# Up-projection: the products A22 T4 of a pair of sets made by seven inner products

## The chip, the cores and the metric

The kernel runs on one core of a Trainium2 chip. The metric is the device time of one launch in microseconds; less is better. On the core, TensorE (PE) multiplies; VectorE (DVE), ScalarE (ACT) and GpSimd (POOL) do elementwise work; SyncE (SP) issues nearly all the transfers.

## The reference

One inference step of a one-layer encoder in float32 on 1024 prompt frames and 32 new ones, 1056 columns in all. The part that the change touches is the up-projection of the squared-ReLU MLP:

```python
f = jnp.square(jax.nn.relu(rmsnorm(x, g_ffn) @ w_up)) @ w_down   # D_MODEL 1024, D_FF 4096
x = x + f
```

## The kernel before

Activations lie with channels on the 128 partitions and the 1056 columns along them. A float32 product is made of three matmuls on rounded values: every operand is split into a high part (a cast on ACT, `copy`) and a low part (source less high part, a subtraction on VectorE), and the kernel adds high x high, high x low and low x high.

**Sets and sevens.** The 4096 outputs of the up-projection are 16 sets of 256. A set's product is a 2 x 2 block product: outputs in two halves of 128, the 1024 inputs in two halves of 512 (four tiles of 128 each), the columns in two halves of 528. It is made from seven block products instead of eight: A11 B11, S1 T1, S2 T2, S3 T3, S4 B22, A12 B21 and A22 T4, where the S are sums of weight blocks (made by GpSimd in `prepare`, split on ACT and VectorE) and the T are sums of activation blocks, made and split once. Each block product runs in two quarters of the columns (264), 12 matmuls a quarter: 4 input tiles x 3. Results gather in PSUM banks: a bank that held A11 B11 is copied out (p1), S2 T2 is added into it, it is copied out again (u2), S3 T3 is added, the difference to S1 T1 (s5) is taken (m2), and A22 T4 is added. VectorE and ACT make the blocks m1 and m2 from the banks; then come Relu, square, a store (`mdB`), and sums of blocks for the down-projection (`mid_sums`: tiles ta and tb, stores to `mdT`).

**Pairs.** Sets 0 and 1 run alone (`seven_late`, `seven`). Sets 2 to 15 run as seven pairs (`seven_pair`). Of a pair one of the seven, A12 B21, is taken for both sets together, and as it is again a 2 x 2 block product (two sets, two halves of the inputs, two quarters), it too is made by seven inner products (`inner_product`, 6 matmuls each: 2 tiles x 3) in place of 48 matmuls. The activations for that, `inner_t` and `low_t`, stay in SBUF. The other six products of both sets take 12 x 2 quarters each, so a pair has 6 x 48 + 42 = 330 matmuls of 264 columns.

**What sets the order.** It is written out by hand. Every product yields when its matmuls are emitted, and `run` then takes one step of each generator in `side`: `prepare` for the next sets (each with a table of steps at which a cast stands; its low part follows a step later), `prepare_inner`, the hooks behind a finished block (`up_hooks`: Relu, square, store, sums), the loads. An engine takes its instructions in the order emitted, so what stands ahead on VectorE, ACT or SP and waits holds up all behind it. Activation tiles come from one pool `blk` of 37 buffers; a new tile waits until all reads of its buffer's last tile are done, transfers from it among them.

Names that the text uses: shS2/slS2 are the high and low part of S2; `raw_u9r` a weight tile of set 9; `td[k]` the DRAM copy of T(k+1), from which the fetches `rt` bring T3 and T4 back at set 0.

Of the kernel before, what the change touches and what calls it, by code (L numbers as in the profile page):

```python
# [15 lines left out]
P = 128  # L16
# [59 lines left out]
def tile_step(  # L76
# [109 lines left out]
        nc.scalar.copy(d[:, 0, :], src)  # L186
        dve(d[:, 1, :], src, d[:, 0, :].bitcast(F32), op=sub)

    def half_w(src, name):
        h, l = (wpool[0].tile([P, 4, P], F32R, tag=f"s{x}", name=f"s{x}{name}", bufs=SHB) for x in "hl")  # L190
        nc.scalar.copy(h, src)  # L191
        return (h, l), partial(dve, l, src, h.bitcast(F32), op=sub)

# [62 lines left out]
    def prepare_inner(key, odd):  # L256
# [38 lines left out]
        low()  # L295
        yield

    def inner_operands(name, g, load):
# [48 lines left out]

    def inner_product(name, w, b, p_=None, pool_=None):

        o = {"B11": low_t[0][0], "B21": low_t[1][0], "B22": low_t[1][1]}.get(b) or inner_t[b]  # L350
        new = p_ is None
        if new:
            p_ = group(f"ps_in{name}", TQ, pool_)
        on = dict(skip_group_check=not new)
        wh, wl = w
        for k in range(2):
# [120 lines left out]
                done("near")  # L477
        done("21")

    def seven_pair(s0, s1, key, m, last, after=({}, {})):  # L480

        def tile_of(k, i):
            return wpool[0].tile([P, TQ], F32, tag=k, name=f"{k}_{s0}{i}")
# [13 lines left out]
        def done(i, k):  # L497
            after[i].get(k, int)()
# [27 lines left out]
        def sixth(i, t):  # L526
            product(i, "A22", "T4", t, x[i][t])
            last(m(i, 1), q[t][1], x[i][t])

        for f in (first, second, third, fourth):  # L530
            for t in range(2):
                f(0, t)
                yield
# [39 lines left out]
        for f, ts_, k in ((third, (1, 0), ""), (fourth, (1, 0), "22"), (fifth, (0, 1), "12")):  # L573
            for t in ts_:
                f(1, t)
                yield
            done(1, k)
        for t in (1, 0):
            sixth(1, t)
            yield  # L580
            done(1, "near" if t else "21")
        for k in (s0, s1, key):
            ws.pop(k)

# [15 lines left out]
            partial(fetch_second, f"{nm}{b}r", w, nb),  # L600
        )

    def ahead_of(nm, a, n):

        e, o = f"{nm}{a}e", f"{nm}{a}o"
        return after(n, prepare(f"{nm}{a}", (6, 8, 10, 11, 14, 16), (e, o, 0))), after(n + 3, prepare_inner(f"{nm}{a}y", o))

    def pair_side(nm, a, b, then=None):

        order = ("S1", "A11", "S2", "S3", "S4", "A22")  # L610
        side.append(after(3, prepare(f"{nm}{b}", (4, 6, 8, 10, 13, 15), (f"{nm}{a}e", f"{nm}{a}o", 1), order)))
        if then:
            for n, f in zip((6, 8, 10, 19), pair_loads(nm, *then)):
                side.append(after(n, call(f)))
            side.extend(ahead_of(nm, then[1], 14))

    def run(body):

# [172 lines left out]
    def md(k, s_):  # L791
# [8 lines left out]
    cvd = dpool.tile([4, 2, P, T], F32, name="cvd")  # L800
    ed = dpool.tile([KD, P, T], F32, name="ed")
    edt = dpool.tile([P, 2, 2 * P], F32, name="edt")
    inner_s = {
        (k, p): {a: dpool.tile([P, NP_, P], F32, name=f"di{k}{p}{a}") for a in ("S1", "S2", "S3", "S4")}
        for k in NESTED for p in range(2)
# [938 lines left out]
        dve(tb[:, 0, :], m2[:, a], ta[:, 1, :], op=sub)  # L1744
        nc.sync.dma_start(md("T4", s_), tb[:, 0, :])

    def up_hooks(i, s_, m):

        def later_(*fs):
            for f in fs:  # L1750
# [31 lines left out]
    def up_pair(a, b):  # L1782
        ms = {}

        def m(i, j):
            if (i, j) not in ms:
                ms[i, j] = blk(f"m{j + 1}_{(a, b)[i]}")
            return ms[i, j]

        return seven_pair(  # L1790
            f"u{a}", f"u{b}", f"u{a}y", m, relu2, [up_hooks(i, (a, b)[i], partial(m, i)) for i in range(2)]
        )

    def up_source(a, b):
# [781 lines left out]
```

## Time and profile before

| | |
|---|---|
| runs | 1510.48, 1510.98 and 1512.48 us, median 1510.98 |
| the profiled execution | 1510.11 us |
| its span, first to last instruction | 1508.4 us |
| mean granted TensorE clock | 0.999 |
| matmuls in the trace | 11556 |
| up-projection, sets 2 to 15 | 789.05 to 1072.76 us, seven pairs of about 40.3 us |

All times of instructions and windows are microseconds from the span's start. In a row of a window stand, behind its bounds, its length; then for PE, PE's weight loads (PEld), DVE, ACT and POOL the busy time with the count of instructions; then the granted clock (1.00 is full), the share of the transfer engines and GB/s. In an order in time a row has start, duration, engine, line, operation, output and inputs, and in brackets idle time ahead of it with what ended it. In a row of a group stand busy time, mean ns and idle time ahead of it; in a row of transfers the count, KB of each and the median time from issue to landing.

### The profile page before, as it was taken

What the parts mean: (1) busy time and instruction counts of PE and PEld (TensorE: products, weight loads), DVE (VectorE), ACT (ScalarE), POOL (GpSimd) and SP (SyncE); (2) the same over time, 40 slices, a digit from 0 to 9 for tenths busy, and PEclk for the clock granted to TensorE, in tenths of its full rate; (3) what the DMA queues carried; (4) which work ended last, traced back from release to release, by engine and by line L of the source; (5) the groups of instructions that cost most, each with busy time, mean ns of one, the idle gap of its engine ahead of it and who ended that gap; (6) DMA issues with size and microseconds to landing.
All of it is one profiled execution on the core that took longest, in us unless ns stands there. A gap on an engine that the chain in (4) does not pass through costs nothing.

```text
span 1508.4 us, 29451 instructions
## 1 busy us (share of the span) xinstructions
PE 1495.6 (99%) x11556; PEld 1481.3 (98%) x11556; DVE 1149.1 (76%) x1628; ACT 794.6 (53%) x1575; POOL 377.7 (25%) x330
## 2 busy tenths in 40 slices
PE   9999999999999999999999999999999999999997
PEld 9999999999999999999999999999999999999997
DVE  6867788879578989876786676666688878879766
ACT  7654444445467767433475555555655433334655
POOL 0434334444121222003324333332000000000251
PEclk9999999999999999999999999999999999999999
DMA  6624425423688766655644434444979767855443
GB/s 242 213 74 171 169 57 198 156 84 98 226 265 251 199 157 154 221 181 184 230 151 146 148 129 144 157 157 150 322 280 284 245 192 238 289 185 166 142 129 123
DMA packets 117259, 275.52 MB, mean 183 GB/s; under 512 B 14048, under 2 KB 31072, under 8 KB 117120
## 3 DMA queue, kind: packets, MB, share of 16 engines
q1 hardware_dynamic: 112144, 259.39, 50.9%
q0 software_dynamic: 1728, 6.29, 2.5%
q10 hardware_dynamic: 3248, 7.96, 1.6%
q8 instruction: 91, 1.49, 0.4%
q14 instruction: 48, 0.39, 0.1%
HBM read 196.10 MB, written 85.88 MB: 187 GB/s over the span
## 4 chain that ended last, share of the span: by engine, by line
PE 93%; DVE 4%; issue 1%; ACT 1%; DMA 1%; ACTq 0%; DVEq 0%; SPq 0%
PE ps_dn L2016 6%; PE ps_dn L2015 6%; PE ps_dn L2014 6%; PE ps_A11i L374 5%; PE ps_A11i L373 5%; PE ps_A11i L375 5%; PE ps_A11u L374 4%; PE ps_A11u L373 4%; PE ps_A11u L375 4%; PE av L1294 2%; PE ps_S1i L375 2%; PE ps_S1i L374 2%; PE ps_S1i L373 2%; PE ps_wo L135 2%; PE ps_wo L133 2%; PE ps_wo L134 2%
## 5 line engine op out<-in xcount | busy, mean ns | idle before, releaser
L2016 PE MATMUL ps_dn<-fhP,wlo_dn 128*128 128x264 f32 x768 | 218.9, 285 | 0.0
L2015 PE MATMUL ps_dn<-flP,whi_dn 128*128 128x264 f32 x768 | 218.7, 285 | 0.1
L2014 PE MATMUL ps_dn<-fhP,whi_dn 128*128 128x264 f32 x768 | 218.2, 284 | 0.0
L2015 PEld LDWEIGHTS ps_dn<-flP,whi_dn 128*128 128x128 f32 x768 | 144.4, 188 | 0.4 <-DVE flP L1880 0.4
L2016 PEld LDWEIGHTS ps_dn<-fhP,wlo_dn 128*128 128x128 f32 x768 | 144.6, 188 | 0.2 <-DVE wlo_dn L1864 0.2
L2014 PEld LDWEIGHTS ps_dn<-fhP,whi_dn 128*128 128x128 f32 x768 | 144.6, 188 | 0.0
L1239 DVE TENSOR_TENSOR_SCAN r<-r 128x128 f32<-128x128 f32 (+3 forms) x64 | 86.8, 1356 | 5.3 <-POOL r L1232 5.3
L2229 POOL TENSOR_TENSOR xx<-xx,pgs 128x400 f32<-128x400 f32 (+1 forms) x17 | 20.0, 1183 | 281.1 <-DVE pgs L2228 281.1
L373 PE MATMUL ps_A11i<-T,shS_i 128*128 128x264 f32 x288 | 82.4, 286 | 0.0
L374 PE MATMUL ps_A11i<-T,shS_i 128*128 128x264 f32 x288 | 82.2, 285 | 0.0
L375 PE MATMUL ps_A11i<-T,slS_i 128*128 128x264 f32 x288 | 81.9, 284 | 0.0
L373 PE MATMUL ps_A11u<-T,shS_u 128*128 128x264 f32 x256 | 73.3, 286 | 0.0
L374 PE MATMUL ps_A11u<-T,shS_u 128*128 128x264 f32 x256 | 72.9, 285 | 0.0
L375 PE MATMUL ps_A11u<-T,slS_u 128*128 128x264 f32 x256 | 72.8, 284 | 0.0
L1232 POOL TENSOR_SCALAR_AFFINE_SELECT r<-r 128x128 f32<-128x128 f32 x64 | 35.9, 562 | 131.9 <-ACT r L1225 131.8
L1858 ACT CAST whi_dn<-raw_dn 128x1024 fp32r<-128x1024 f32 x31 | 32.6, 1052 | 66.9 <-PE ps_dn L2015 54.7
L1880 DVE TENSOR_TENSOR flP<-mrP,fhP 128x1056 fp32r<-128x1056 f32 x48 | 59.9, 1252 | 6.2 <-ACT fhP L1875 6.2
L135 PE MATMUL ps_wo<-mh,wlo_wo 128*128 128x352 f32 x192 | 62.0, 323 | 0.0
L134 PE MATMUL ps_wo<-ml,whi_wo 128*128 128x352 f32 x192 | 61.9, 322 | 0.0
L133 PE MATMUL ps_wo<-mh,whi_wo 128*128 128x352 f32 x192 | 61.6, 323 | 0.0
L251 DVE TENSOR_TENSOR slS_i<-s_i,shS_i 128x512 fp32r<-128x512 f32 x54 | 48.2, 892 | 13.1 <-ACT shS_i L191 12.8
L1279 DVE TENSOR_TENSOR at<-pa,at 128x512 fp32r<-128x512 f32 (+2 forms) x96 | 50.4, 548 | 9.3 <-ACT at L1278 8.4
(1711 smaller groups left out, 5789.0 us busy)
## 6 DMA issues: line engine op xcount, KB each, us to landing
raw_dn<-in_w_down_dram SPq DMA_DIRECT2D x59, 512.0 KB, 5.3
mrP<-mdT SPq DMA_DIRECT2D x32, 528.0 KB, 6.1
mdB<-m SPq DMA_DIRECT2D x48, 264.0 KB, 2.1
mrP<-mdB SPq DMA_DIRECT2D x24, 528.0 KB, 6.7
s<-gd SPq DMA_DIRECT2D x16, 528.0 KB, 5.4
mdT<-ta SPq DMA_DIRECT2D x32, 264.0 KB, 2.9
raw_pg<-in_w_ple_gate_dram SPq DMA_DIRECT2D x15, 512.0 KB, 3.5
gd<-m_i SPq DMA_DIRECT2D x12, 528.0 KB, 2.9
```

Source lines behind the costliest of these rows:

```text
L133: nc.tensor.matmul(ps, wh, xh[k][:, cols], start=(k == order[0]), stop=False)
L134: nc.tensor.matmul(ps, wh, xl[k][:, cols], start=False, stop=False)
L135: nc.tensor.matmul(ps, wl, xh[k][:, cols], start=False, stop=(k == order[-1]))
L373: nc.tensor.matmul(p_, wh[:, k, :], h, start=new and n == 0, stop=False, **on)
L374: nc.tensor.matmul(p_, wh[:, k, :], l, start=False, stop=False, **on)
L375: nc.tensor.matmul(p_, wl[:, k, :], h, start=False, stop=z, **on)
L1239: nc.vector.tensor_tensor_scan(rev, rev, rev, 1.0, ALU.mult, ALU.bypass)
L1279: nc.vector.tensor_tensor(al, pt[:, :nb, :], ah.bitcast(F32), op=ALU.subtract)
L1880: dve(l, mraw.pop(v), opd[v].bitcast(F32), op=sub)
L2014: nc.tensor.matmul(ps, hi[:, j, :], oh, start=j == 0, stop=False)
L2015: nc.tensor.matmul(ps, hi[:, j, :], ol, start=False, stop=False)
L2016: nc.tensor.matmul(ps, lo[:, j, :], oh, start=False, stop=j == NP_ - 1)
```

## The change

For the pairs from set 4 on, A22 T4 is also taken for both sets together and made by seven inner products: 42 matmuls in place of 48. Its weights are split by the new `prepare_last` (high and low parts in the tiles lw for A11|A12, lx for S1|S3, ly for S2|S4, and a small pair for A22), its sums of weights are made on VectorE. Its activations are seven blocks of T4, made once beside sets 2 and 3 by `last_operands` from the DRAM copy of T4, split, and stored to DRAM (`zd`); every pair loads each of them again, 528 KB, when it needs it (`z_load`, tiles zt). T4's last part gets a DRAM copy for that (`td[3][3]`). The pair's products stand in a new order (`seven_both`): each inner product beside a product of the sets, its result copied or subtracted into a tile `tmp` or added straight into the set's bank (`outer`), or added to m2 in SBUF (`fold`). As one quarter of m2 is now finished in SBUF, its Relu reads SBUF in a hook (`c21`).

```diff
-    def half_w(src, name):
-        h, l = (wpool[0].tile([P, 4, P], F32R, tag=f"s{x}", name=f"s{x}{name}", bufs=SHB) for x in "hl")
+    def half_w(src, name, n=4):
+        h, l = (wpool[0].tile([P, 4, P], F32R, tag=f"s{x}", name=f"s{x}{name}", bufs=SHB)[:, :n, :] for x in "hl")
...
+    def prepare_last(key, a, b):
+        ra, rb = (raws[f"{x}r"][:, 4:8, :] for x in (a, b))
...
+        low = pair_of(ra, "lw", ("A11", "A12"))
+        yield
+        low()
+        yield
+        s = blk(f"ls{key}", F32, [P, 8, P])
+        s1, s3, s2, s4 = (s[:, 2 * i : 2 * i + 2, :] for i in range(4))
+        dve(s1, rb[:, 0:2, :], rb[:, 2:4, :], op=add)
+        dve(s3, ra[:, 0:2, :], rb[:, 0:2, :], op=sub)
+        low = pair_of(s[:, 0:4, :], "lx", ("S1", "S3"))
+        yield
+        dve(s2, s1, ra[:, 0:2, :], op=sub)
+        low()
+        yield
+        dve(s4, ra[:, 2:4, :], s2, op=sub)
+        low = pair_of(s[:, 4:8, :], "ly", ("S2", "S4"))
+        yield
+        low()
...
+        w["A22"], low = half_w(rb[:, 2:4, :], f"a{key}", 2)
...
+    def last_operands(nm, load):
+        raw = [blk(f"rl{nm}{k}", F32, [P, 2, TH]) for k in range(2)]
...
+        sums_ = ((3, 3, 1, sub), (1, 0, 1, sub), (0, 0, 3, add), (2, 2, 0, sub))
+        for (o, a, b, op), kind in zip(sums_, ("T3", "T1", "T2", "T4")):
+            for k in range(2):
+                dve(x[k][o], x[k][a], x[k][b], op=op)
...
+                for k in range(2):
+                    nc.scalar.copy(d[:, 0, k, :], x[k][i])
+                yield
+                for k in range(2):
+                    dve(d[:, 1, k, :], x[k][i], d[:, 0, k, :].bitcast(F32), op=sub)
+                nc.sync.dma_start(zd[nm][name], d.bitcast(F32))
...
+    def z_load(nm, b):
+        zt[b] = t = blk(f"zt{b}", F32R, [P, 2, 2, TQ])
+        nc.sync.dma_start(t.bitcast(F32), zd[nm][b])
...
+        def outer(a, b, on=None, pool_=few):
+            return inner_product(f"l{a}{key}", ws[f"{key}l"][a], zt.pop(b), on, pool_)
+        def fold(i, t, by):
+            dve(m(i, 1)[:, q[t][1]], x[i][t], by, op=add)
+        def seven_both():
+            for f in (first, second):
+                for t in range(2):
+                    f(0, t)
+                    yield
...
+            xl = outer("A11", "B11", pool_=tps)
+            nc.scalar.copy(p4, xl)
+            third(0, 0)
+            yield
+            z_load(both, "T2")
+            third(0, 1)
+            yield
+            zl = outer("S1", "T1")
+            nc.scalar.copy(s4, zl)
+            fourth(0, 0)
+            yield
+            z_load(both, "B21")
+            fourth(0, 1)
...
+            outer("S2", "T2", xl)
+            dve(v4, xl, s4, op=sub)
...
+            outer("A12", "B21", x[0][0])
+            fold(0, 0, p4)
...
+            outer("S4", "B22", x[0][1])
+            fold(0, 1, v4)
...
+            outer("S3", "T3", xl)
...
+            fourth(1, 0)
+            yield
+            done(1, "22")
+            fifth(1, 0)
+            outer("A22", "T4", x[1][0])
+            fold(1, 0, u4)
...
+            if more:
+                z_load(more, "T1")
...
         def c21():
-            side.append(later_(partial(done, 1, 0, "B21")))
+            fs = (partial(done, 1, 0, "B21"),)
+            side.append(later_(*((partial(relu2, m(1), halves[0]),) if both else ()), *fs))
...
             raw_t[KD // 2 - 1] = sums(KD // 2 - 1, e, o)
+            nc.sync.dma_start(td[3][KD // 2 - 1], raw_t[KD // 2 - 1]["T4"])
...
-            pair_side("u", a, a + 1, up_source(a + 2, a + 3) if more else None)
+            pair_side("u", a, a + 1, up_source(a + 2, a + 3) if more else None, a > 2, more)
+            if a == 2:
+                side.append(after(1, last_operands("u", lambda to, j: nc.sync.dma_start(to, td[3][j]))))
```

How the order moves, first on ACT and VectorE at the front of sets 8 and 9. Names with u8 or _8 are set 8's, those with 7 the set's before it; whi1_u8y and wlo1_u8y are weights of the old inner products; lw, lx, ls are the new ones. On ACT before, from the Relu of set 7 to the square that ends the stretch:

```order
L1726 ACTIVATE m2_7_11724<-ps_A11u7_0_11624 128x264
L191 CAST shS2_u8_11817<-s2_u8_11612 128x512
L1726 ACTIVATE m1_7_11608<-m1_7_11608 128x528
L506 COPY p1_u80_11835<-ps_A11u8_0_11822 128x264
L191 CAST shS3_u8_11838<-s3_u8_11613 128x512
L1729 ACTIVATE m1_7_11608<-m1_7_11608 128x528
```

and now, from set 8's first eviction:

```order
L582 COPY p1_u80_11937<-ps_A11u8_0_11924 128x264
L305 CAST lwu8yl_11939<-raw_u8r_11540 128x512
L267 CAST whi1_u8y_11810<-si_u8y_11808 128x512
L1920 ACTIVATE m2_7_11851<-m2_7_11851 128x528
L1917 ACTIVATE m2_7_11851<-m2_7_11851 128x528
L1917 ACTIVATE m1_7_11720<-m1_7_11720 128x528
L582 COPY p1_u81_11960<-ps_A11u8_1_11947 128x264
L191 CAST shS2_u8_11963<-s2_u8_11724 128x512
L1920 ACTIVATE m2_7_11851<-m2_7_11851 128x528
L1920 ACTIVATE m1_7_11720<-m1_7_11720 128x528
```

The cast of S2 has moved from two rows ahead of set 8's first eviction to seven behind it, and two squares follow it. On VectorE before:

```order
L251 TENSOR_TENSOR slS1_u8_11783<-raw_u8r_11430,shS1_u8_11782 128x512
L290 TENSOR_TENSOR wlo1_u8y_11685<-si_u8y_11681,whi1_u8y_11683 128x512
L251 TENSOR_TENSOR slS2_u8_11818<-s2_u8_11612,shS2_u8_11817 128x512
L251 TENSOR_TENSOR slS3_u8_11839<-s3_u8_11613,shS3_u8_11838 128x512
L1735 TENSOR_TENSOR ta7_11858<-m1_7_11608 128x528
```

and now:

```order
L251 TENSOR_TENSOR slS1_u8_11920<-raw_u8r_11540,shS1_u8_11919 128x512
L311 TENSOR_TENSOR lwu8yl_11939<-raw_u8r_11540,lwu8yl_11939 128x512
L290 TENSOR_TENSOR wlo1_u8y_11812<-si_u8y_11808,whi1_u8y_11810 128x512
L1926 TENSOR_TENSOR ta7_11970<-m1_7_11720 128x528
L315 TENSOR_TENSOR lsu8yl_11989<-raw_u9r_11855 128x256
L316 TENSOR_TENSOR lsu8yl_11989<-raw_u8r_11540,raw_u9r_11855 128x256
L251 TENSOR_TENSOR slS2_u8_11964<-s2_u8_11724,shS2_u8_11963 128x512
L1929 TENSOR_TENSOR m1_7_11720<-m2_7_11851,m1_7_11720 128x528
L319 TENSOR_TENSOR lsu8yl_11989<-lsu8yl_11989,raw_u8r_11540 128x256
L320 TENSOR_TENSOR lxu8yl_11992<-lsu8yl_11989,lxu8yl_11992 128x512
L251 TENSOR_TENSOR slS3_u8_11996<-s3_u8_11725,shS3_u8_11995 128x512
```

ta of set 7, which reads ACT's square of m1, stood behind the low parts of S2 and S3 and now stands ahead of both, with two sums between. Second, on SP at set 0 now (before, the row of L2585 isn't there, and the rest is the same):

```order
L1877 DMA xd_140<-xr7_9448 128x1056
L2585 DMA td3_145<-xr7_9448 128x528
L1836 DMA rt01_9755<-td2_144 128x528
L1836 DMA rt01_9755<-td3_145 128x528
L1836 DMA rt11_9758<-td2_144 128x528
L1836 DMA rt11_9758<-td3_145 128x528
L1836 DMA rt21_9761<-td2_144 128x528
L1836 DMA rt21_9761<-td3_145 128x528
```

The store reads T4's fourth part, which VectorE makes in place in xr7; the six fetches stand behind it. Third, on VectorE beside sets 2 and 3 now, where rl are the raw halves of T4, z the split blocks and L362 their low parts; none of the L348 and L362 rows are there before:

```order
L362 TENSOR_TENSOR zT3u_10397<-rlu0_10302,zT3u_10397 128x264
L362 TENSOR_TENSOR zT3u_10397<-rlu1_10303,zT3u_10397 128x264
L596 TENSOR_TENSOR m2_2_10412<-ps_A11u2_1_10280,s5_u21_10348 128x264
L717 TENSOR_TENSOR p1_u20_10276<-ps_inA11u2y_10439,p1_u20_10276 128x264
L600 TENSOR_TENSOR m1_2_10459<-u2_u20_10369,ps_S1u2_0_10314 128x264
L251 TENSOR_TENSOR slS1_u3_10434<-raw_u3r_9952,shS1_u3_10433 128x512
L362 TENSOR_TENSOR zT1u_10436<-rlu0_10302,zT1u_10436 128x264
L362 TENSOR_TENSOR zT1u_10436<-rlu1_10303,zT1u_10436 128x264
```

and five rows on:

```order
L362 TENSOR_TENSOR zT2u_10486<-rlu0_10302,zT2u_10486 128x264
L362 TENSOR_TENSOR zT2u_10486<-rlu1_10303,zT2u_10486 128x264
L348 TENSOR_TENSOR rlu0_10302<-rlu0_10302 128x264
L348 TENSOR_TENSOR rlu1_10303<-rlu1_10303 128x264
L732 TENSOR_TENSOR m1_2_10459<-ps_inA12u2y_10538,p1_u20_10276 128x264
L251 TENSOR_TENSOR slS2_u3_10530<-s2_u3_10353,shS2_u3_10529 128x512
L362 TENSOR_TENSOR zT4u_10534<-rlu0_10302,zT4u_10534 128x264
L362 TENSOR_TENSOR zT4u_10534<-rlu1_10303,zT4u_10534 128x264
L738 TENSOR_TENSOR p1_u22_10563<-ps_inA11u2y_10439,s5_u22_10497 128x264
```

The evictions of sets 2 and 3 (L596, L600, L717, L738) now stand between the steps that make the blocks. On TensorE there are 36 matmuls less in the whole program.

More of the change, by code (lines that the diff above doesn't have):

```diff
@@ L348, in inner_product @@
     def inner_product(name, w, b, p_=None, pool_=None):
-        o = {"B11": low_t[0][0], "B21": low_t[1][0], "B22": low_t[1][1]}.get(b) or inner_t[b]
+        o = b
+        if isinstance(b, str):
+            o = {"B11": low_t[0][0], "B21": low_t[1][0], "B22": low_t[1][1]}.get(b) or inner_t[b]
         new = p_ is None
         if new:
-            p_ = group(f"ps_in{name}", TQ, pool_)
+            p_ = group(f"ps_in{name}", TQ, pool_) if pool_ is not tps else tps.tile([P, 512], F32, tag="tp", name=f"ps_in{name}")[:, :TQ]
         on = dict(skip_group_check=not new)
@@ L478, in seven_late, with seven_pair @@
         done("21")
-    def seven_pair(s0, s1, key, m, last, after=({}, {})):
+    def seven_pair(s0, s1, key, m, last, after=({}, {}), both=None, more=None):
         def tile_of(k, i):
@@ L530, in seven_pair @@
+        if both:
+            yield from seven_both()
+            return
         for f in (first, second, third, fourth):
@@ L577, in seven_pair @@
             done(1, k)
+        if more:
+            z_load(more, "B11")
         for t in (1, 0):
@@ L581, in seven_pair @@
             done(1, "near" if t else "21")
+        if more:
+            z_load(more, "T1")
         for k in (s0, s1, key):
@@ L614, in pair_side @@
                 side.append(after(n, call(f)))
-            side.extend(ahead_of(nm, then[1], 14))
+            side.extend(ahead_of(nm, then[1], 14, more))
     def run(body):
@@ L802, in tile_step @@
     edt = dpool.tile([P, 2, 2 * P], F32, name="edt")
+    zd = {
+        nm: {k: dpool.tile([P, 2, 2, TQ], F32, name=f"zd{nm}{k}") for k in ("B11", "B21", "B22", "T1", "T2", "T3", "T4")}
+        for nm in ("u",)
+    }
     inner_s = {
@@ L1745, in mid_sums, with up_hooks @@
         nc.sync.dma_start(md("T4", s_), tb[:, 0, :])
-    def up_hooks(i, s_, m):
+    def up_hooks(i, s_, m, both=False):
         def later_(*fs):
@@ L1788, in m @@
             return ms[i, j]
+        both = a > 2
         return seven_pair(
-            f"u{a}", f"u{b}", f"u{a}y", m, relu2, [up_hooks(i, (a, b)[i], partial(m, i)) for i in range(2)]
+            f"u{a}", f"u{b}", f"u{a}y", m, relu2, [up_hooks(i, (a, b)[i], partial(m, i), both) for i in range(2)],
+            "u" if both else None, "u" if a + 2 < NSET else None,
         )
```

103 lines of the change are left out of this document (99 added, 4 removed).

## The prediction

> **What bounds the kernel now.** I read the page's busy times first, then a table of windows with one window for each pair of sets, then the orders in time of the engines at the front of one pair, sets 8 and 9.
>
> ```profile
> PE 1495.6 (99%) x11556; PEld 1481.3 (98%) x11556; DVE 1149.1 (76%) x1628; ACT 794.6 (53%) x1575; POOL 377.7 (25%) x330
> PE 93%; DVE 4%; issue 1%; ACT 1%; DMA 1%; ACTq 0%; DVEq 0%; SPq 0%
> ```
>
> TensorE holds 93% of the chain that ended last. The stage that changes is the up-projection; its windows per pair (sets 4-5, then 8-9), and sets 8-9 cut in two behind the first 11.7 us:
>
> ```profile
> 829.36:869.63 40.27, 40.27 (x333) 40.27 (x332) 25.49 (x38) 21.94 (x47) 14.92 (x12) 1.00 0.43 147
> 911.67:951.94 40.27, 40.27 (x333) 40.27 (x331) 25.60 (x41) 21.96 (x47) 15.31 (x12) 1.00 0.43 147
> 911.67:923.35 11.68, 11.68 (x99) 11.68 (x97) 11.14 (x13) 7.59 (x17) 6.57 (x4) 1.00 0.42 136
> 923.35:951.94 28.59, 28.59 (x237) 28.59 (x235) 14.45 (x29) 14.37 (x30) 8.75 (x8) 1.00 0.43 152
> ```
>
> Two things stand here. A pair takes 40.27 us, in which the program has 330 products of 264 columns (the counts take in a neighbour or two): **0.122 us a product**, without a gap. So the pair is TensorE's alone. But VectorE's 25.60 us are not spread evenly: 11.14 of the first 11.68 us are busy, and 14.45 of the other 28.59. Work added at a pair's front finds no room there.
>
> **What goes.** Per changed pair 48 products of A22 T4 become 7 x 6 = 42. Six pairs change: 6 x 6 = 36 products x 0.122 = **-4.4 us**, the whole gain. Everything else must be hidden to keep it.
>
> **The low part of S2, five times.** This is the place of the order fences of sets 8-9. The rows of before there, 911.67 being set 8's first product:
>
> ```profile
> 911.67 0.28 PE L373 MATMUL ps_A11u<-B,shA_u 128*128 128x264 f32 x1
> 912.15 0.61 ACT L191 CAST shS_u<-s_u 128x512 fp32r<-128x512 f32 x1
> 912.66 0.65 ACT L1726 ACTIVATE m<-m 128x528 f32<-128x528 f32 x1
> 913.31 0.38 ACT L506 COPY p_u<-ps_A11u 128x264 f32<-128x264 f32 x1
> 913.59 0.62 ACT L191 CAST shS_u<-s_u 128x512 fp32r<-128x512 f32 x1
> ...
> 911.52 0.42 DVE L286 TENSOR_TENSOR wlo_u8y<-raw_u8o,whi_u8y 128x256 fp32r<-128x256 f32 x1
> 911.86 0.68 DVE L251 TENSOR_TENSOR slS_u<-raw_u8r,shS_u 128x512 fp32r<-128x512 f32 x1
> 912.46 0.68 DVE L290 TENSOR_TENSOR wlo_u8y<-si_u8y,whi_u8y 128x512 fp32r<-128x512 f32 x1
> 913.06 0.68 DVE L251 TENSOR_TENSOR slS_u<-s_u,shS_u 128x512 fp32r<-128x512 f32 x1
> 914.25 1.21 DVE L251 TENSOR_TENSOR slS_u<-s_u,shS_u 128x512 fp32r<-128x512 f32 x1 [0.50 <-ACT shS_u L191]
> 915.37 1.79 DVE L1735 TENSOR_TENSOR ta<-m 128x528 f32<-128x528 f32 x1
> 917.20 1.68 DVE L1738 TENSOR_TENSOR m<-m,m 128x528 f32<-128x528 f32 x1
> 918.80 1.77 DVE L295 TENSOR_TENSOR wlo_u8y<-raw_u8o,whi_u8y 128x512 fp32r<-128x512 f32 x1
> 920.50 0.70 DVE L1741 TENSOR_TENSOR ta<-m 128x528 f32<-128x528 f32 x1
> ...
> 913.22 1.68 POOL L253 TENSOR_TENSOR s_u<-raw_u8e,raw_u9r 128x512 f32<-128x512 f32 x1 [6.70 <-DVE wlo_u8y L290]
> 914.98 1.62 POOL L253 TENSOR_TENSOR raw_u9r<-raw_u9r 128x512 f32<-128x512 f32 x1
> 918.39 1.64 POOL L253 TENSOR_TENSOR s_u<-s_u,raw_u8o 128x512 f32<-128x512 f32 x1
> ```
>
> From row to row an engine steps by a little less than a duration: ACT 0.52 for a cast of 512 columns (912.15 to 912.66), 0.55 for 528, 0.28 for an eviction (913.31 to 913.59); VectorE 0.60 for 512, 0.34 for 256. Before, the low part of S2 (913.06 + 0.68) is out 2.07 us behind the front; TensorE wants it at its 51st product, 50 x 0.122 = 6.1. It leads by 4.0 us.
>
> Now, ACT from the first eviction, which stays at 913.31 - 911.67 = 1.64: eviction 0.28, cast of A11|A12 0.52, cast for the inner weights 0.52, a square 0.55, two Relus 1.10 (one is new: set 7's last quarter pair used to get its Relu while it was evicted), eviction 0.28, cast of S2 0.52, square 0.55, square 0.65: ends at 6.61. VectorE's subtraction ta reads that last square, and now stands ahead of the low part of S2. Behind it: ta 0.62, two sums of 256 columns 0.34 each, the low part 0.68: out at 8.6. The new inner product A11 B11 puts TensorE's need back by 6 products, to 56 x 0.122 = 6.83. TensorE waits **1.75 us** if no row is stretched. The rows from 914.25 to 918.80 show VectorE's instructions at 1.2 to 1.8 us while GpSimd's four sums run, 0.68 to 0.70 otherwise. GpSimd's second sum would run at about 5.7 to 7.3 here, beside half of ta: some 0.35 more, 2.1 us. Were all four stretched as those rows are, 4.5. I take 2.1, nearest to the rows, for the five pairs whose predecessor is also changed (sets 6, 8, 10, 12, 14): **+10.5** (8.75 to 22).
>
> **The rest of such a pair.** The wait gives VectorE time, but not enough. From 8.87 stand ahead of the sum for S4: a subtraction 0.62, a sum 0.34, two low parts 1.20, ta 0.62, and the sum 0.42, to 12.1; GpSimd's last two sums, let go by S2's low part, run beside them, and at the rows' stretch cost about 2 us: 14.1. ACT's cast for S2|S4 waits for that sum, and behind it stand another cast and the eviction of u2's second quarter: 0.52 + 0.52 + 0.38 later, 13.5 to 15.5. TensorE, restarted at 8.95, wants that bank 40 products on, at 13.8: 0 to 1.7, taken as 0.9. Second, the load of B22 (30 products between its place and its use, 3.7 us):
>
> ```profile
> raw_u8r<-in_w_up_dram SPq DMA_DIRECT2D x1, 512.0 KB, 4.8
> gd<-m_i SPq DMA_DIRECT2D x12, 528.0 KB, 2.9
> mdT<-ta SPq DMA_DIRECT2D x32, 264.0 KB, 2.9
> ```
>
> A weight tile of about this size takes 4.8 us to land, and SP can run ahead of its place only as far as the queue's earlier rows let it: 0 to 1.1, taken as 0.5. Third, at the pair's end 12 products (1.5 us) stand between the last S3 T3 and the inner A22 T4 that is added into the same bank, whose eviction follows four or five VectorE instructions: 0 to 0.7, taken as 0.5. Together 1.9 a pair: **+9.5** (0 to 17.5). Over the whole pair VectorE stays below TensorE: 25.6 us, and three low parts of 512 and one of 256 columns, four sums of 256 and some adds from PSUM more, two low parts of 512 less, about 30 of 39.5 us; it is the front that overflows.
>
> **The first changed pair** (sets 4-5) has no changed predecessor; the loads and the eviction remain: **+2.5** (0 to 3.8).
>
> **Making the operands**, beside sets 2-3 (third order fence). T3, T1, T2, T4 leave one after the other, and the build puts m1 of set 2 into T3's buffer, so its first eviction waits until T3's store has landed; T2's casts wait for T1's store, T4's for T2's. A store of 528 KB takes 2.9 us (row gd). From T3's low part to the sum p1 that TensorE waits for: 2.9, eviction 0.35, low part 0.60, T1 low 0.76, 2.9, T2 casts 0.66, low 0.76, 2.9, T4 casts 0.66, low 0.76, p1 0.43 = 13.7. TensorE wants p1 at its 205th product, 24.9. T3's low part must be out by 11.2; it stands behind an eviction that TensorE only lets go at 10.4 (84 products and 0.16), so 10.8 + 0.76 = 11.6 at best, and ahead of both stand tb of set 1 and m2 of set 2, whose buffers wait for mdT stores of 2.9 us. **+5** (0.4 to 7).
>
> **The queue at set 0** (second order fence). The new store of T4's fourth part stands on SP ahead of six fetches:
>
> ```profile
> 749.19 3.16 SPq L1645 DMA_DIRECT2D rt<-td  x6
> 752.54 0.76 DVE L182 SCALAR_TENSOR_TENSOR xr<-xr,vecT,w 128x528 f32<-128x528 f32 x1
> rt<-td SPq DMA_DIRECT2D x12, 264.0 KB, 4.3
> 756.34 0.64 ACT L186 CAST T<-rt 128x528 fp32r<-128x528 f32 x1
> 757.28 1.17 ACT L186 CAST T<-rt 128x528 fp32r<-128x528 f32 x2
> 761.54 0.37 ACT L463 COPY u_u<-ps_A11u 128x264 f32<-128x264 f32 x1
> ```
>
> What it stores is ready at 753.30, so the fetches go from 753.6 in place of 749.19. The fifth lands at 753.6 + 4 x 0.53 + 4.3 = 760.0, its cast was at 757.8: ACT is 2.2 us later, and the eviction at 761.54 with it. Some of that is lead. **+1.5** (0 to 4).
>
> **The down-projection's start.** The tail of set 15 puts more on VectorE just where it makes the first operands, and TensorE already waits there:
>
> ```profile
> L2015 PEld LDWEIGHTS ps_dn<-flP,whi_dn 128*128 128x128 f32 x768 | 144.4, 188 | 0.4 <-DVE flP L1880 0.4
> ```
>
> No row prices it: 0 to 5, taken as **+3**, the order of one stretched low part of 1.25 us twice.
>
> **The sum.** -4.4 + 10.5 + 9.5 + 2.5 + 5 + 1.5 + 3 = +27.6. The profiled execution took 1510.11 us (span 1508.4 and 1.7 around it), the median is 1510.98: 1510.98 + 27.6 = 1538.6, **1539**.
>
> **Rivals.** *All hidden*: only the 36 products count, 1506.6. It decides at S2's low part: out within 6.83 us, which needs ACT through its ten instructions 1.8 us sooner than their rows allow, or ta behind S2 as before. For it speaks VectorE's idle half of the last 28.6 us of a pair; against it that the order is fixed and the idle time lies behind the wait. *The S2 wait alone*: TensorE's own waiting gives the other queues and loads their time back; -4.4 + 8.75 to 10.5 + 1 to 3 for the stores: 1516 to 1520, say 1518. *The clock falls too*:
>
> ```profile
> 1480.00:1500.00 20.00, 19.86 (x168) 19.54 (x166) 14.98 (x34) 13.87 (x31) 0.33 (x1) 1.00 0.36 121
> 1500.00:1508.00 8.00, 0.85 (x9) 0.77 (x7) 3.35 (x11) 3.38 (x5) 0.00 (x0) 0.80 0.34 131
> ```
>
> Where TensorE is all but idle for 8 us, the granted clock was 0.80, and 1.00 in every window above. If a wait of 2 us had that effect for 8 us behind it, each pair would lose 8 x (1/0.80 - 1) = 2 us more, 12 in all: 1551. Against it: a wait of 2 us is a quarter of that idle stretch. [...]
>
> **Chances.** Forecast 0.66, S2 alone 0.2, all hidden 0.07, clock 0.07. Of these, within 0.2% (3 us, about what a measurement of this kernel can tell from no change) are some of the cases in between: 0.03; faster 0.06; slower 0.91. The low ends of all waits but S2's give 1515, all high ends over 1560; 1518 to 1553 leaves out one in ten on each side.
>
> **What would show it.** In the new profile: TensorE idle ahead of S2's low matmul, put down to VectorE, five times by about 2 us, and none at set 4; windows of changed pairs of 43 to 45 us in place of 39.5; waits on p1 and on ACT's evictions beside sets 2-3; the six fetches behind 753 us. Windows of 39.5 us would overthrow it; so would an S2 low part that comes before TensorE's need, or a granted clock below 1.00 in these windows.

## The result and the profile after

Measured on one chip, in turns with the kernel before: 1549.86 us in the median of six runs (1547.66 to 1554.06), against 1511.79 (1510.48 to 1512.64): 38.1 us slower, **ratio 1.0254**, 95% interval 1.024 to 1.0268. The forecast was 1539, its range 1518 to 1553.

The page of the kernel after, engines and the chain that ended last (a chain followed back from the end; it stops here in the down-projection, so its shares don't compare with those of before):

```profile
PE 1500.6 (97%) x11520; PEld 1480.7 (96%) x11520; DVE 1174.5 (76%) x1716; ACT 802.2 (52%) x1601; POOL 378.6 (24%) x330
PE 27%; DVE 1%; ACT 1%; DMA 1%; issue 0%; ACTq 0%; SPq 0%; DVEq 0%
```

TensorE has its 36 products less (11556 to 11520), and is listed as busy for 5 us more than before: in this column a matmul that comes slower counts for longer (at half clock 17 or 18 fill a window of 3.41 us, at full clock 30, 831.81 to 835.22). Where the time went is seen in the windows. Of before, the stretches that aren't in the prediction: set 0, sets 2-3, sets 6-7, and the first 146 products of the down-projection:

```profile
748.03:768.53 20.50, 20.50 (x171) 20.50 (x170) 16.36 (x28) 14.18 (x27) 2.23 (x1) 1.00 0.53 184
789.06:829.36 40.30, 40.30 (x333) 40.30 (x332) 26.56 (x46) 22.24 (x49) 18.64 (x12) 1.00 0.42 145
869.63:911.67 42.04, 42.04 (x339) 41.40 (x338) 34.40 (x53) 21.95 (x47) 15.79 (x12) 1.00 0.39 141
1072.76:1091.02 18.26, 18.09 (x146) 17.67 (x145) 12.58 (x13) 10.07 (x17) 0.00 (x0) 1.00 1.01 363
```

and of after the same stretches by the same first products, with sets 4-5, 8-9 and 14-15:

```profile
748.42:772.95 24.53, 22.53 (x171) 22.10 (x169) 17.12 (x28) 14.37 (x27) 3.21 (x2) 0.93 0.56 188
793.48:844.12 50.64, 43.14 (x332) 42.09 (x331) 31.16 (x62) 24.41 (x57) 17.98 (x12) 0.97 0.52 180
844.12:886.79 42.67, 40.42 (x327) 39.77 (x325) 30.09 (x49) 21.81 (x48) 15.87 (x12) 1.00 0.69 240
886.79:933.40 46.61, 42.07 (x333) 40.66 (x331) 36.91 (x63) 22.82 (x49) 15.02 (x12) 1.00 0.60 210
933.40:976.71 43.31, 40.06 (x327) 39.64 (x326) 28.95 (x52) 22.81 (x49) 15.57 (x12) 1.00 0.64 225
1063.26:1106.58 43.32, 40.07 (x327) 39.65 (x325) 27.77 (x51) 26.34 (x52) 5.82 (x4) 1.00 0.75 255
1106.58:1128.91 22.33, 19.35 (x146) 17.92 (x145) 14.94 (x16) 9.49 (x15) 0.00 (x0) 1.00 0.97 346
```

The differences: set 0 +4.0, sets 2-3 +10.3, sets 4-5 +2.4, 6-7 +4.6, each of the four last pairs +3.0, the start of the down-projection +4.1. Together 37.5, which is the difference of the two spans (1545.9 - 1508.4). Every changed pair is longer than before, though it holds 6 products less, and in none of them is VectorE the fuller engine (28.95 of 43.31 us in sets 8-9). Two windows show a clock below 1.00, and neither holds a changed pair.

Which waits these are, from the view of waits of the kernel after (engine and what it ran, what it waited for; us in all, times, the longest):

```profile
PE ps_A11u L451 <- DVE slS_u L251: 8.2, 5, 1.6
PE ps_A11u L449 <- ACT u_u L592: 7.7, 6, 1.6
PE ps_inA11u2y L433 <- DVE p_u L738: 3.3, 1, 3.3
PE ps_inA12u2y L433 <- DVE m L600: 2.9, 1, 2.9
PE ps_A11u L433 <- DVE m L596: 1.9, 1, 1.9
PE ps_A11u L449 <- ACT u_u L539: 1.9, 1, 1.9
PE ps_dn L2209 <- DVE flP L2074: 1.8, 4, 1.1
PE ps_inlA11u4y L433 <- DMA ztT<-zduT: 1.6, 1, 1.6
```

First row: the low part of S2, five times, as forecast. Second: u2's second quarter. Third and fourth: sets 2-3. Fifth: the end of set 7, once. Sixth: the eviction at set 0. Seventh: the start of the down-projection. Eighth: T2's load in the first changed pair. A wait costs 0.2 to 0.3 us more than it is listed with. At set 8 the first row's wait is listed with 1.63; from product to product (940.12 to 942.04) it is 1.92, less the 0.12 of a product itself 1.80, and the product behind it follows after 0.22 us in place of 0.12.

Two orders in time show the mechanisms. VectorE at the front of sets 8-9, where ta waits for the last square on ACT and S2's low part stands behind it:

```profile
940.00 0.71 DVE L1926 TENSOR_TENSOR ta<-m 128x528 f32<-128x528 f32 x1 [2.70 <-ACT m L1920]
...
941.30 0.68 DVE L251 TENSOR_TENSOR slS_u<-s_u,shS_u 128x512 fp32r<-128x512 f32 x1
```

ta starts 6.60 us behind the pair's first product (forecast 6.61), and the low part is out at 8.58 (forecast 8.6, without the stretching by GpSimd that I added: both run unstretched). And VectorE beside sets 2-3, with the transfer of T3's store as the last row:

```profile
809.95 0.41 DVE L717 TENSOR_TENSOR p_u<-ps_inA11u2y,p_u 128x264 f32<-128x264 f32 x1
815.29 0.43 DVE L600 TENSOR_TENSOR m<-u_u,ps_S1u 128x264 f32<-128x264 f32 x1 [4.93 <-DMA zduT<-zT3u]
...
824.85 1.84 DVE L362 TENSOR_TENSOR zT4u<-rlu,zT4u 128x264 fp32r<-128x264 f32 x2
826.61 0.42 DVE L738 TENSOR_TENSOR p_u<-ps_inA11u2y,s_u 128x264 f32<-128x264 f32 x1
zduT<-zT3u SPq DMA_DIRECT2D x1, 528.0 KB, 5.5
```

m1 of set 2 waits 4.93 us for the store of T3, whose buffer it has been given, and the whole of VectorE's queue with it. That store took 5.5 us to land; the three behind it took 2.6 to 2.8. T4's low parts come at the end of the chain, ahead of the sum p1 that TensorE wants.

The clock, cut at the bounds of the two slow stretches (first two and last two rows; the granted clock stands behind POOL), and the same steps around the wait for m1 of set 2 (third and fourth):

```profile
763.53:766.95 3.41, 1.54 (x13) 1.49 (x13) 2.96 (x7) 3.41 (x9) 0.00 (x0) 1.00 0.38 142
766.95:770.36 3.41, 3.41 (x17) 3.41 (x17) 2.19 (x6) 1.40 (x2) 0.70 (x1) 0.50 0.97 322
811.32:814.73 3.41, 1.56 (x13) 1.35 (x11) 0.00 (x0) 0.77 (x2) 0.00 (x0) 1.00 0.53 213
814.73:818.15 3.41, 2.38 (x18) 2.26 (x18) 2.86 (x8) 0.00 (x0) 0.00 (x0) 1.00 0.09 37
824.97:828.39 3.41, 1.30 (x10) 1.30 (x11) 3.33 (x6) 2.03 (x6) 1.33 (x1) 1.00 0.26 106
828.39:831.80 3.41, 3.41 (x18) 3.41 (x17) 0.43 (x1) 0.66 (x2) 1.27 (x1) 0.50 0.35 136
```

For 3.41 us the clock is 0.50, and about 16 products are begun in place of 28; the lost 12 are 1.5 to 1.6 us. Ahead of each of the two lies a stretch of the same length in which TensorE was busy for less than half (1.54 and 1.30 us). The two begin 61.44 us apart, which is 18 steps of 3.413 us. The third row left about as little work, 1.56 us against the first row's 1.54, and the clock stayed at 1.00.

### The profile page after: what moved, and what is told of

Its sections match the earlier page's. It is cut to its first block, busy times and chain, and to the rows that moved or that the text cites. A ratio compares the mean times of both kernels' runs of the same rounds, so it can differ in the third digit from the quotient of the medians.

```text
span 1545.9 us, 29650 instructions
## 1 busy us (share of the span) xinstructions
PE 1500.6 (97%) x11520; PEld 1480.7 (96%) x11520; DVE 1174.5 (76%) x1716; ACT 802.2 (52%) x1601; POOL 378.6 (24%) x330
## 5 line engine op out<-in xcount | busy, mean ns | idle before, releaser
L449 PEld LDWEIGHTS ps_A11u<-T,shS_u 128*128 128x128 f32 x256 | 48.7, 190 | 11.4 <-ACT u_u L592 9.3
L451 PEld LDWEIGHTS ps_A11u<-T,slS_u 128*128 128x128 f32 x256 | 48.8, 190 | 9.2 <-DVE slS_u L251 9.2
```

The source lines that it names most:

```text
L449: nc.tensor.matmul(p_, wh[:, k, :], h, start=new and n == 0, stop=False, **on)
L451: nc.tensor.matmul(p_, wl[:, k, :], h, start=False, stop=z, **on)
```

## The experiments

**Theory.** The 38 us are waits of TensorE for what the order of the queues (VectorE, ACT, SP) and the reuse of buffers put late, each at its place, plus two stretches at half clock. **Rival**: the added work or transfers fill an engine or the memory, so the time is lost in any order; then a change of order only moves the waits. Each run was measured in turns with the kernel before, whose median was 1510.7 us for the first four, 1512.67 for e5 to e7 and 1511.55 for e8; I compare differences to it. The changed kernel's is +38.1.

### The operands alone, and the store at set 0

e1: no pair uses the new order, all else stays.

```diff
-        both = a > 2
+        both = a >= 98
```

> All eight pairs keep the old order; only the making and storing of the seven operands remains (the store of T4's fourth part at set 0, the eleven stores and the sums beside sets 2-3). The operands are never used. Theory (each stage has its own waits): set 0 costs +4.0 and sets 2-3 +10.4 as in the changed kernel, every later pair is back at 40.27 us, the down-projection starts as before: 1511.8 + 14.4 = 1526. Rival (the waits beside sets 2-3 come from preparing the first changed pair, not from making the operands): only set 0's share, 1516. A time near 1512 would mean that the operands are free by themselves.

Measured 1524.12 us, **+13.4** (ratio 1.0079, 1.0062 to 1.0095). Its windows of set 0, sets 2-3 and sets 8-9:

```profile
748.98:771.82 22.84, 21.26 (x171) 20.62 (x170) 16.55 (x28) 14.38 (x27) 2.18 (x2) 1.00 0.57 191
792.32:840.35 48.03, 41.60 (x333) 40.54 (x331) 30.88 (x62) 24.42 (x57) 17.99 (x12) 1.00 0.54 190
922.64:962.90 40.26, 40.26 (x333) 40.26 (x332) 25.47 (x41) 21.94 (x47) 15.32 (x12) 1.00 0.42 147
```

The waits stand at set 0 and sets 2-3 without any changed pair behind them, and the other pairs are as before. This execution took 1520.97 us and had no slow stretch (+2.3 and +7.7 in the two windows, both at 1.00); the other three took 1523.76 to 1525.04. The first theory holds, and a third of the loss is the making of operands.

e2: the store of T4's fourth part leaves SP's queue.

```diff
-            nc.sync.dma_start(td[3][KD // 2 - 1], raw_t[KD // 2 - 1]["T4"])
...
+                if n == 2:
+                    nc.scalar.dma_start(td[3][KD // 2 - 1], raw_t[KD // 2 - 1]["T4"])
```

> The changed kernel, with the store of T4's fourth part issued by ScalarE behind the third group of its casts, off SyncE's queue; the six fetches stand where they stood before the change. Theory (fetches queued behind the store, then the clock answers the wait): the waits 0.29 and 2.04 us of set 0 go, and the stretch of 3.4 us at half clock behind them with its 1.6 us: 1549.9 - 3.9 = 1546. Rival 1 (the half clock has another cause than the wait): it stays, 1547.6. Rival 2 (the fetches are late because the transfers themselves are slower, not because of the order): 1549.9.

Measured 1545.88 us, **+35.2**, 2.9 less than the changed kernel. Set 0, then two stretches at set 7:

```profile
748.80:769.29 20.49, 20.49 (x169) 20.49 (x169) 16.35 (x28) 14.18 (x27) 2.33 (x1) 1.00 0.65 217
923.54:926.95 3.41, 1.52 (x12) 1.31 (x12) 3.27 (x7) 0.65 (x1) 0.93 (x2) 1.00 0.41 159
926.95:930.36 3.41, 3.41 (x18) 3.41 (x17) 2.75 (x6) 0.00 (x0) 0.00 (x0) 0.50 0.94 313
```

Set 0 is back at 20.5 us, 4.0 less: the order on SP was the cause, and the half clock went with the wait. But a stretch at half clock now stands behind the wait at the end of set 7, which the changed kernel has too, there at full clock. The same wait is followed by half clock in one run and not in the other; that made me test the clock by itself (e9, e10).

### The front of a pair: later sums, an earlier load, a later cast

e3: S2's low part ahead of ta again.

```diff
-                side.append(after(2, mid_sums(s_, m(0), m(1))))
+                side.append(after(3 if both else 2, mid_sums(s_, m(0), m(1))))
```

> The changed kernel, with the sums of the finished set (ta, tb and two others on VectorE) emitted one step later in the pairs that use the new order, so that S2's low part stands ahead of ta again. Theory: the wait for S2's low part, 1.8 us five times, falls to 0.5 or less: -6.5 to -9, and the time that TensorE no longer idles is missing elsewhere: the second quarter of u2 and the loads come relatively earlier on TensorE, which takes back 2 to 5: about 1544. Rival 1 (nothing takes its place): 1541. Rival 2 (all of it comes back, since the front of a pair has too much VectorE work in any order): 1549.9, with TensorE's waits moved to other instructions of the same stretch.

Measured 1546.03 us, **+35.3**, only 2.8 less. Its waits:

```profile
PE ps_A11u L451 <- DVE slS_u L251: 2.2, 5, 0.4
PE ps_inlA11u12y L433 <- DMA ztT<-zduT: 1.8, 1, 1.8
PE ps_inlA11u8y L433 <- DMA ztT<-zduT: 0.9, 1, 0.9
PE ps_inlA11u14y L433 <- DMA ztT<-zduT: 0.9, 1, 0.9
```

S2's wait falls from 8.2 to 2.2 us; but now T2's load is late in five of the six changed pairs (by 1.4 us in sets 4-5 and 0.6 in sets 10-11 too), where it was late in the first alone. TensorE's wait for S2 had covered it. The expectation named u2 and the loads as what comes back; it was the loads, and they gave back most of it.

e4: as e3, and T2's load one step earlier.

```diff
+            z_load(both, "T2")
             xl = outer("A11", "B11", pool_=tps)
             nc.scalar.copy(p4, xl)
             third(0, 0)
             yield
-            z_load(both, "T2")
```

> As the run before, and T2's load is placed one step (18 products, 2.2 us) earlier in each of the six pairs. Theory (a load has a fixed lead, and the S2 wait gave it more): the first changed pair loses its wait of 1.8 us for T2, and each of the others what the run before shows on T2's load: 2 to 9 us below the run before, 1535 to 1542. Rival (the transfers are limited by bandwidth, so that an earlier place brings no earlier landing): the same time as the run before, within 1 us.

Measured 1540.0 us, **+29.3**: 6.0 less than e3, and no wait for T2 is left. Sets 4-5, the first changed pair, in e4 (42.67 us in the changed kernel, 40.27 before):

```profile
843.31:884.24 40.93, 40.33 (x327) 39.76 (x325) 29.17 (x49) 21.85 (x48) 16.22 (x12) 1.00 0.73 251
```

The load is limited by its place, not by bandwidth: the core moves 251 GB/s here, against 240 in the changed kernel's window, and the load comes in time. Two other loads are now late once each: B22's by 0.6 us in sets 12-13 and B21's by 1.1 us in sets 14-15.

e6: as e4, and the cast of S2|S4 one step behind the sum for S4.

```diff
         dve(s4, ra[:, 2:4, :], s2, op=sub)
+        yield
         low = pair_of(s[:, 4:8, :], "ly", ("S2", "S4"))
```

> The kernel of the earlier run with both the later sums and T2's earlier load, 1540.0 us, and in addition ScalarE's cast of S2|S4 for the outer set is emitted one step after the sum for S4, so that it stands behind the eviction of u2's second quarter. Theory (ScalarE is held by a cast that waits for VectorE): the wait of 1.8 us on that eviction, five times, goes, and VectorE, which then runs later relative to TensorE, gives back about 1 us a pair at the next low part or load: 1540 - 9 + 5 = 1536. Rival 1 (nothing comes back): 1531. Rival 2 (VectorE's front is the limit, all comes back elsewhere in the same pair): 1540.

Measured 1537.47 us, **+24.8**, 4.5 less than e4. The first row of its waits, and sets 12-13:

```profile
PE ps_S1u L452 <- DVE slS_u L251: 6.2, 5, 1.3
1012.11:1053.83 41.72, 40.02 (x327) 39.60 (x326) 30.61 (x52) 22.88 (x49) 15.78 (x12) 1.00 0.70 234
```

The wait for u2, 7.7 us in all in the changed kernel, is gone. In its place TensorE waits five times for another low part on VectorE, that of S4. So both theories are right here, each for a part: the order was bad, and the front of a pair holds more VectorE work ahead of that low part than there is time for. VectorE works from 1014.69 to 1028.3 us of this pair with no gap above 0.1 us. Four of the instructions in this stretch are the finished set's sums (ta, tb and two others); whether they could stand behind S4's low part was not tried. The pair stands 1.5 us above the 40.27 of before, in place of 3.0.

### The chain of stores beside sets 2-3

e5 leaves out the four stores of T3, T1, T2 and T4, and loads B11's stored quarter where one of these four is wanted, so some products are formed with other operands.

```diff
-                nc.sync.dma_start(zd[nm][name], d.bitcast(F32))
...
-        nc.sync.dma_start(t.bitcast(F32), zd[nm][b])
+        nc.sync.dma_start(t.bitcast(F32), zd[nm][b if b[0] == "B" else "B11"])
```

> The changed kernel without the four stores of T3, T1, T2 and T4 beside sets 2-3; the sums, casts and low parts are still made. The later loads of these four read B11's stored quarter instead, so the amount loaded is the same and the products of the outer sets are formed with other operands. Theory (buffers come free only when a store has landed, and what waits for them is queued ahead of what TensorE waits for): the waits 3.05, 0.35, 0.64 and 3.43 us beside sets 2-3 go, the 0.83 on the first p1 stays, and with the wait of 3.43 the half clock behind it goes: sets 2-3 take 42 us in place of 50.65, 1549.9 - 9 = 1541. Rival (the sums and casts themselves fill VectorE and ScalarE): the waits stay, 1550.

Measured 1542.04 us, **+29.4**, 8.7 less than the changed kernel. Sets 2-3:

```profile
794.70:835.92 41.22, 40.55 (x333) 40.34 (x332) 28.53 (x59) 24.34 (x57) 18.56 (x12) 1.00 0.51 168
```

41.22 us in place of 50.64, with the same sums and casts on VectorE and ACT: the chain of stores through reused buffers was the cause, and only the 0.8 us on the first p1 is left. This execution too has two stretches at half clock: the one beside sets 2-3 is gone, but one now stands in sets 4-5 behind T2's late load (1.9 us), so the whole program gained less than this window.

### The last pair alone

e7: only sets 14-15 use the new order (`both = a >= 14`).

> Only the last pair, sets 14-15, uses the new order; its operands are made beside sets 2-3 as in the changed kernel, and pairs 4-5 to 12-13 stay as before the change. Theory (terms add up by place): the operands' 13.4 us of the run with no changed pair (1524.1), a changed pair without a changed pair ahead of it +2.4 as sets 4-5 show, and the start of the down-projection +4.0: 1530.5, with no wait for S2's low part. Rival (the down-projection starts late because VectorE and the loads are behind from pair to pair): 1526.5, its start as before the change.

Measured 1532.77 us, **+20.1**, so 6.7 above e1; forecast 6.4. Sets 14-15, and the same 146 products of the down-projection as above:

```profile
1050.19:1093.06 42.87, 40.44 (x326) 39.76 (x325) 28.78 (x48) 25.34 (x51) 6.18 (x4) 1.00 0.80 271
1093.06:1115.37 22.31, 19.34 (x146) 17.91 (x145) 15.04 (x16) 9.61 (x15) 0.00 (x0) 1.00 0.96 347
```

A changed pair without one ahead of it takes 42.9 us (42.67 at sets 4-5), without a wait for S2, and the down-projection starts as late as with six changed pairs (22.33). For this start nothing piles up from pair to pair; the tail of the last pair is enough.

### All that helped

e8 takes e6, the store on ScalarE (one step later than in e2) and `last_operands` begun one step earlier (`after(0, ...)`).

> All edits that helped, together (later sums, T2's earlier load, later cast of S2|S4: 1537.5 us), with the store of T4's fourth part on ScalarE (-4.0 in its own run), and the making of the operands begun one step (12 products, 1.5 us) earlier beside sets 2-3. Theory (the places add up): 1537.5 - 4.0 - 2 to 4 for the chain of stores, which stays as long but starts sooner: 1530 to 1532. Rival (the chain of stores only moves its waits from p1 to an earlier eviction): 1533.5. Neither comes near the kernel before (1511 to 1513): what is left is the chain, a VectorE wait in every pair's front and the start of the down-projection.

Measured 1533.89 us, **+22.3** (ratio 1.0151, 1.0134 to 1.0168): 2.5 less than e6, where 5.5 to 7.5 were expected. Set 0 is at 20.50 us; but of the 4.0 us expected there 1.6 were a stretch at half clock, which e6's profile does not have at set 0. And beside sets 2-3, 47.62 us, the rival came true: the chain's wait moved to the first p1:

```profile
PE ps_inA11u2y L434 <- DVE p_u L718: 3.8, 1, 3.8
```

No version that was run beats the kernel before.

### The clock by itself

e9 and e10 are the kernel before, in which ScalarE copies out u2's second quarter several times in place of once, so that TensorE waits once a pair.

```diff
-            nc.scalar.copy(u2[i][t], x[i][t])
+            for _ in range({("u2", 0, 1): 9, ("u4", 0, 1): 10, ...}.get((s0, i, t), 1)):
+                nc.scalar.copy(u2[i][t], x[i][t])
```

> The kernel before, in which ScalarE evicts the second quarter of u2 of the first set of a pair 9, 10, 11, 12, 13, 14 and 15 times in place of once (sets 2, 4, 6, 8, 10, 12, 14; the same values each time). One more eviction is 0.28 us and the lead is 0.9, so TensorE waits once a pair, for about 1.3, 1.6, 1.9, 2.2, 2.4, 2.7 and 3.0 us, or more if a copy that rewrites a tile steps slower. Theory (the clock is judged over fixed stretches of 3.413 us, and the next one is run at half clock where TensorE idled 1.9 us or more of one): none behind waits below 1.8 us, some but not all behind those of 2 to 3 us, according to how the wait lies to the stretches; every stretch at half clock lasts 3.4 us, starts a whole number of 3.413 us after another, and costs 1.6 us: 1511.8 + 15.1 + 2 to 5 of 1.6 = 1530 to 1535. [...] Rival 2 (it is the length of the wait alone that decides): half clock behind every wait over one length.

Measured once, 1547.9 us. A copy that rewrites its tile stepped by 0.41 us here (12 in 4.89), not 0.28, so the waits were longer than meant: 2.46, 2.87, 2.87, 3.69, 4.10, 4.51 and 4.92 us from product to product, less the 0.12 of a product. Behind **all seven** stands a stretch at clock 0.50 (the mean granted clock of this execution is 0.988, of the kernel before 0.998 and 0.999). So 2.46 us were enough, and it is open whether length alone decides.

> As the run before with seven waits, but shorter: eight evictions in sets 2, 4, 6, 8, 10 and seven in sets 12 and 14. In the run before an extra eviction took 0.41 us, and nine made a wait of 2.46 us, so these are waits of 2.05 us (five) and 1.64 us (two). Theory (fixed stretches of 3.413 us, judged by the idle time in each): of the five, those that lie within one stretch, about half, are followed by half clock, the others and the two shorter ones are not; two half-clock stretches start a whole number of 3.413 us apart; time 1511.6 + 13.5 + 1 to 4 of 1.6 = 1527 to 1531.5. Rival (the length of the wait alone decides, with a bound somewhere between 1.8 and 2.46 us): the five of 2.05 us behave alike, all with half clock (1533) or none (1525).

Measured once, 1528.09 us (the kernel before in the same measurement 1514.28). The waits are 2.06, 2.05, 1.64, 2.06, 2.05 and twice 1.64 us. Behind the second and the fifth stands half clock, behind the others not. The two with the stretch behind them, and the stretches that hold the greater part of the first, third and fourth wait:

```profile
842.27:845.68 3.41, 1.52 (x12) 1.31 (x12) 1.49 (x4) 3.22 (x9) 0.00 (x0) 1.00 0.96 252
845.68:849.09 3.41, 3.41 (x18) 3.41 (x17) 1.18 (x3) 1.56 (x3) 0.00 (x0) 0.50 0.62 214
971.97:975.39 3.42, 1.53 (x13) 1.32 (x12) 1.57 (x3) 3.20 (x10) 0.00 (x0) 1.00 0.94 255
975.39:978.80 3.41, 3.41 (x18) 3.41 (x17) 1.12 (x2) 1.77 (x4) 0.00 (x0) 0.50 0.62 223
...
801.30:804.72 3.42, 2.17 (x17) 2.17 (x18) 0.49 (x2) 2.17 (x5) 2.17 (x2) 1.00 0.16 14
886.64:890.05 3.41, 2.11 (x15) 1.55 (x14) 2.87 (x7) 3.20 (x9) 0.00 (x0) 1.00 0.68 228
931.01:934.43 3.42, 1.86 (x15) 1.86 (x16) 1.14 (x4) 2.65 (x7) 0.00 (x0) 1.00 0.76 281
```

All windows are cut on one grid of 3.413 us, laid through the slow stretches (845.68 and 975.39 are 38 steps apart). Where a wait of 2.05 us fell into one step and left TensorE busy for 1.52 or 1.53 us of it, the next step ran at half clock; where it was split by a bound and left 1.86 or more, it didn't. Of four waits of 2.05 to 2.06 us two were followed by half clock and two were not, so length alone did not decide. e1's profile shows the same with a longer wait. The wait for p1 beside sets 2-3 is listed there with 3.3 us, as in the changed kernel, where half clock follows it; in e1 a bound of the grid splits it into steps with 1.80 and 1.70 us of work, and the clock stays at 1.00:

```profile
819.72:823.13 3.41, 1.80 (x15) 1.59 (x14) 2.23 (x4) 2.74 (x8) 2.64 (x3) 1.00 0.56 223
823.13:826.55 3.41, 1.70 (x14) 1.70 (x15) 2.94 (x5) 1.97 (x5) 1.37 (x2) 1.00 0.38 156
```

## Why the prediction came out as it did

The mechanism was right and the sum 10 us too small. Term by term, from the windows:

| term | forecast | measured |
|---|---|---|
| 36 products less | -4.4 | -4.4 (11520 against 11556) |
| S2's low part, five times | +10.5 | +9.0 (5 x 1.8) |
| the rest of these pairs | +9.5 | +11.4 (16.7 longer, + 3.7 of products, - 9.0) |
| first changed pair | +2.5 | +3.1 (2.4 longer, and its 0.7 of products) |
| operands beside sets 2-3 | +5 | +10.3 |
| the queue at set 0 | +1.5 | +4.0 |
| start of the down-projection | +3 | +4.1 |

- **S2's low part**: right in place, cause and count. ACT's ten instructions and VectorE's four ran as summed; only the 0.35 us for GpSimd was too much. e3 shows the cause (8.2 to 2.2 us).
- **The rest of the pair**: the wait for u2 was taken as 0.9, the middle of 0 to 1.7, and measured 1.7 in the mean, its upper end; the load of B22, taken as 0.5, is in no row of the changed kernel (it is late once in e2, by 1.1 us, and once in e4, by 0.6); the end's eviction came once, 2.05 us at set 7, not five times 0.5. The sum is near, its parts are not: that it is near is luck. That VectorE's front overflows is shown by e6, where the wait passes on to S4.
- **First changed pair**: its size was near. The late load was T2's (1.8 us), not B22's, which was the one that I had priced.
- **Operands**: the step that was most mis-sized. The chain of stores was the right cause (e5), but it was longer than summed. From T3's low part (out at 809.68, 16.2 us behind the first product of set 2) to p1 (827.03) it took 17.35 us against 13.7. With the summed 13.7 that start gives 16.2 + 13.7 - 24.9 = 5.0, the +5 as taken; but T3's store took 5.5 us to land where I had put 2.9, and the low parts of T4, priced at 0.76, took 1.84 beside GpSimd. These 3.7 us and the half clock, 1.6, are the 5.3 that the term is short. TensorE met the chain in two places, m1 of set 2 and p1, where I had let it wait at p1 alone; with the smaller ones beside them the waits came to 8.3 us, over my upper end of 7. Why T3's store was slow was not tested; it was issued 1.7 and 1.3 us behind two weight loads that took 5.4 us in the median.
- **Set 0**: the later fetches were right (e2), and I took lead for granted that wasn't there: 2.3 us of wait and 1.6 of half clock.
- **Down-projection**: taken without a row, 3 for 4; e7 shows that the last pair makes it. Six waits of TensorE there, 2.9 us as listed, are put down to VectorE's low parts and one cast on ACT; which instruction of the last pair makes these late was not tried.
- **Rivals**: all hidden never came near. "The S2 wait alone" fails by e1: 13.4 us lie where no pair is changed. "The clock falls too" I gave 0.07, as a loss in every pair. It was partly so: of the 38 us two stretches of 1.6, at sets 0 and 3. Against it I had put that a wait of 2 us is a quarter of the 8 us at the program's end in which the clock was 0.80. The length was no measure: 2.04 us were enough at set 0 and 2.05 in e10, each with 3.41 us at clock 0.50 behind it, and behind two other waits of 2.06 us in e10 the clock stayed at 1.00.

## What to carry to other kernels

A change that trades TensorE work for work on other engines is priced at the stretch where that work must be done, not over the stage: here VectorE was idle for 14 of 43 us in a pair and still late at its front. Before a DRAM round trip is put beside a running stage, follow which tile gets the stored buffer next: here its first writer, m1 of set 2, waited 4.93 us for the landing, and VectorE's whole queue with it. And when one wait is taken away, look at which load or eviction it had covered: three of the edits here (e3, e6, e8) moved a good part of the wait that they removed.

## What was not expected of the hardware

A wait of TensorE cost more here than its length where it left too little work in one step of a grid of 3.413 us: the next step ran at clock 0.50 and lost some 12 products, about 1.5 us. The grid is read from the changes of the granted clock in each profiled execution. In the changed kernel's they lie at 766.95, 770.36, 828.39 and 831.80 us and, behind the last product, at 1541.77: from one to the next 1, 17, 1 and 208 steps of 3.4133 us. Laid so over all twelve profiles, from 740 to 1140 us, it shows a bound: each of the 22 steps at full clock in which TensorE was busy for 1.54 us or less was followed by a step at half clock, and none of the steps with 1.56 us or more was. So the bound in these profiles lies at about 1.55 of the 3.413 us, by the profile's busy times, in which the ends of matmuls are modelled. A step that was already at half clock was followed by a second one where TensorE was busy for 2.6 us or less of it (four cases), and by full clock where it was busy for 2.9 or more.

The grid did not start with the program: a step begins 2.36 us behind the first instruction in the changed kernel's profile, 1.17 us behind it in e9's and 2.57 us in e10's. And the executions of one kernel differ: the mean granted clock of the changed kernel's six is 0.995 to 0.997, of e5's four 0.996 to 0.999, where one such stretch takes 0.001 of it. That the steps lie differently in each execution is a possible reason for the wider scatter of the changed kernel (6.4 us over six runs, against 2.2 for the kernel before in the same measurement), but it was not tested, and the kernel before alone scattered by up to 4.0 us over seven runs in a later measurement.
